# Rotary halves 32 partitions apart: swapping them with ScalarE copies out of PSUM instead of SBUF DMAs, with the products in natural token order

## Chip, cores, metric

The kernel runs as one program on the 8 cores of a Trainium2 chip; each core owns 2048 of 16384 tokens. The metric is the device time in microseconds (us) of the slowest core. Some executions fall into a slow state, in which one die runs at a visibly lower granted clock (0.81 to 0.96 instead of 0.98) and takes up to 18% longer. The engines are TensorE (PE), VectorE (DVE), ScalarE (ACT), GpSimd (POOL) and SyncE (SP, which only issues DMAs here).

## The reference, cut to what matters

```python
def apply_partial_rope(t, cos, sin):          # first 32 of 128 head dims
    half = ROT_DIM // 2                        # 16
    t1, t2, rest = t[..., :half], t[..., half:ROT_DIM], t[..., ROT_DIM:]
    return jnp.concatenate([t1 * cos - t2 * sin, t1 * sin + t2 * cos, rest], axis=-1)
...
q = apply_partial_rope(q.reshape(B, S, N_QKV_HEADS, HEAD_DIM), cos, sin)
k = apply_partial_rope(k.reshape(B, S, N_QKV_HEADS, HEAD_DIM), cos, sin)
# 3 groups of 8 heads; dilations 1, 4, 16; windows of 128 strided keys
```

The rest (norm, modulation, dilated attention, gated convolution, output projection) is untouched.

## The kernel before

A core first makes the values (called the first stage below), then projects and rotates the keys of the 2048 tokens in front of its own (the **halo stage**), then does its own heads with their attention (the **own stage**), then convolution and output. Head dims lie on partitions, tokens on the free axis. Rotation needs the two halves of 16 dims exchanged, so that both factors of a product lie on the same partitions; the kernel before exchanges them by two SBUF-to-SBUF DMAs per call:

```python
# kernel before, cut
def rope(pv, g, buf, off, T, n, tab, tc, rings, lag=2):
    R = DIL[g]                                   # 1, 4, 16
    if g == 2:
        dv = buf.all()                           # four token blocks T, one dependency
        dap = buf.ap.rearrange("p (r m) -> p r m", r=16)[:, :, 32 * T:32 * T + 32]
    ...
    S.op("act", copy(out=dap, in_=iv(pv.ap)), reads=[pv], writes=[dv])               # cast
    S.op("dve", t1 = pv[0:32] * table[0:32], reads=[pv, tv], writes=[t1])            # first product
    S.dmas("sp", [(sw[32:48], dap[16:32]), (sw[48:64], dap[0:16])], reads=[dv], writes=[sw])
    def tail():                                  # two slots later
        S.op("dve", t2 = sw[32:64] * table[32:64], ...)                              # second product
        S.op("pool", dap[0:32] = t1 + t2, reads=[t1, t2], writes=[dv])               # add
    at(clock[0] + lag, 0, tail)
```

`iv` and `fv` view tokens in residue order (all tokens with the same remainder by the dilation together), the order in which the attention wants them. Dependencies are kept per 256-byte cell of the views named in `reads` and `writes`.

The host plans the order of each engine's instructions. It simulates all engines with estimated durations (`op_cost`; for DMAs an issue time plus about 2.1 us) and emits each engine's list in the simulated order of start. Each engine then has its instructions in that order, so an estimate that is off can make it wait at one instruction while later ones are ready.

```python
if nd.nbytes:
    issue = (0.55 if e == "pool" else 0.1) * len(nd.items)   # planner: us per DMA issued
```

The softmax here doesn't subtract the row's maximum and nothing guards it: scores larger than these inputs give would overflow.

Of the kernel before, what the change touches and what calls it, by code (L numbers as in the profile page):

```python
# [6 lines left out]
F32 = mybir.dt.float32  # L7
# [272 lines left out]
def op_cost(eng, fn):  # L280
    p = Probe()
    fn(p)
    name, k = p.got
    if eng == "pe":
        n = _free(k["rhs"]) if "rhs" in k else 128
        c = max(n, 120) / 2.4e3 + 0.004
        if name == "matmul" and k["rhs"].dtype == F32:
            c *= 4
        return c
    out = k["out"]  # L290
    ins = [v for key, v in k.items() if key in ("in_", "in0", "in1") and v is not None]
    n = max(_free(a) for a in ins)
    ps = any("PS" in str(a.space) for a in ins + [out])
    ptr = any(hasattr(k.get(key), "ap") for key in ("scale", "bias", "scalar", "scalar1"))
    far = n > 64 and any(len(a.ap) > 2 and a.ap[-1][0] not in (0, 1) for a in ins + [out])
    if eng == "act":
        return (n + (190 if ps else 240)) / 1.2e3 + (0.1 if ptr else 0.0)
    if eng == "pool":
        return (2.5e-3 if far or out.shape[0] > 32 else 2.2e-3) * n + 0.1
    f = 1.0  # L300
    if name in ("tensor_copy", "tensor_scalar"):
        b2 = all(a.dtype == BF16 for a in ins + [out])
        f = 1.0 if ps else (4.0 if b2 else 2.0)
    elif name == "tensor_tensor" and not ps and all(a.dtype == BF16 for a in ins + [out]):
        f = 1.5
    elif name == "reciprocal":
        f = 0.167
    if n < 16:
        return 0.26
    return (n / f * (1.5 if far else 1.0) + 151) / 0.96e3 + (0.05 if ptr else 0.0)  # L310
# [10 lines left out]
class Sched(Emit):  # L321
# [66 lines left out]
    def _plan(self):  # L388
# [26 lines left out]
        while count < len(nodes):  # L415
            best = None
            for e in ENGS:
                o = order[e]
                h = head[e]
                while h < len(o) and done[o[h]]:  # L420
                    h += 1
                head[e] = h
                cand = None
                seen = 0
                j = h
                win = self.WIN[e]
                while j < len(o) and seen < win:
                    nd = nodes[o[j]]
                    j += 1
                    if done[nd.idx]:  # L430
                        continue
                    seen += 1
                    if nd.left:
                        continue
                    st = max(free[e], nd.ready)
                    if nd.nbytes:
                        st = max(st, dma_free - 5.0)
                    k = (st, nd.idx if e == "pe" else nd.need, nd.idx)
                    if cand is None or k < cand[0]:
                        cand = (k, nd)  # L440
                if cand is not None and (best is None or (cand[0][0], cand[1].need) < (best[0][0], best[1].need)):
                    best = cand
            (st, _, _), nd = best
            e = nd.eng
            nd.start = st
            done[nd.idx] = True
            count += 1
            if nd.nbytes:
                issue = (0.55 if e == "pool" else 0.1) * len(nd.items)
                free[e] = st + issue  # L450
                b = max(dma_free, st + issue + 1.0)
                dma_free = b + max(nd.nbytes / 340e3, 0.1)
                end = dma_free + 1.0
            else:
                end = st + nd.cost
                free[e] = end
                end += 0.15
            for j in nd.succs:
                s = nodes[j]
                s.left -= 1  # L460
                if s.ready < end:
                    s.ready = end
# [57 lines left out]
def build_program():  # L520
    nc = bass.Bass("TRN2", target_bir_lowering=False)
    xt_d = nc.dram_tensor("xt", [8, 128, 16 * 512], F32, kind="ExternalInput").ap()
    crow_d = nc.dram_tensor("crow", [128, D], F32, kind="ExternalInput").ap()
    pos_d = nc.dram_tensor("pos64", [64, HALO + TOK], I32, kind="ExternalInput").ap()
    cf_d = nc.dram_tensor("cstf", [128, NCF], F32, kind="ExternalInput").ap()
    cb_d = nc.dram_tensor("cstb", [128, NCB], F32, kind="ExternalInput").ap()
    wada_d = nc.dram_tensor("wada", [3, 16, 128, D], F32, kind="ExternalInput").ap()
# [35 lines left out]
    with ExitStack() as st:  # L563
# [39 lines left out]

        stage = [S.buf(TL + 32768 + 4096 * i, [4, 4, 128], BF16) for i in range(2)]
        stats = [S.buf(TL + 40960 + 256 * i, [8], F32) for i in range(4)]
        tkv = S.buf(TL, [TOK], F32, parts=64)
        NW = 3
        wring = [S.buf(TL + 4096 * i, [KC, 128], BF16) for i in range(NW)]
        hring = wring + [S.buf(TL + 28672 + 4096 * i, [KC, 128], BF16) for i in range(3)]
# [1 line left out]
        def wslot(j):  # L611
            return hring[j % 6] if j < 24 else wring[j % NW]

        tab_o = S.buf(TL + 12288, [TOK], F32, parts=64)
        tab_h = S.buf(TL + 20480, [HALO], F32, parts=64)
        t1s = [S.buf(TL + 20480 + 2048 * i, [512], F32, parts=32) for i in range(3)]
        t2s = [S.buf(TL + 26624, [512], F32, parts=32), S.buf(R1 + 63232, [512], F32, parts=32)]
        sws = [S.buf(TL + 28672 + 1024 * i, [512], BF16, parts=64) for i in range(3)]
        zw = S.buf(TL + 31744, [KC, 128], BF16)
        F1, F2, F3 = [S.buf(TL + 35840 + 2048 * i, [512], F32) for i in range(3)]  # L620
        kth = [S.buf(R0 + 5376 * i, [2688], BF16) for i in range(2)]
        t1h = [S.buf(R0 + 10752 + 2048 * i, [512], F32, parts=32) for i in range(4)]
        t2h = [S.buf(R0 + 18944 + 2048 * i, [512], F32, parts=32) for i in range(4)]
        swh = [S.buf(R0 + 27136 + 1024 * i, [512], BF16, parts=64) for i in range(4)]
        q2 = S.buf(R1, [TOK], BF16)
        k2 = S.buf(R1 + 4096, [TOK], BF16)
        kh2 = [S.buf(R1 + 8192 + 1024 * i, [4, 128], BF16) for i in range(2)]
# [386 lines left out]
        def table_steps(tb, p0):  # L1014
# [8 lines left out]
                         reads=[in_, cf.all()], writes=[out])  # L1023
                steps.append(f)
            steps.append(lambda: S.dma("pool", tb.ap, pos_d[:, p0:p0 + 2048], writes=[sv]))
            ts(sv, sv, cf.ap[0:64, CF_INVF:CF_INVF + 1], None, ALU.mult)
            ts(kv, sv, inv2pi, MAGIC, ALU.mult, ALU.add)
            ts(kv, kv, MAGIC, None, ALU.subtract)
            for Cc in (C1, C2):
                steps.append(lambda Cc=Cc: S.op("dve", lambda e: e.scalar_tensor_tensor(  # L1030
                    out=sv.ap, in0=kv.ap, scalar=-Cc, in1=sv.ap, op0=ALU.mult, op1=ALU.add), reads=[kv, sv], writes=[sv]))
            ts(sv, sv, PI_LO, -PI_LO, ALU.min, ALU.max)
            steps.append(lambda: S.op("act", lambda e: e.activation(out=tb.ap, in_=tb.ap, func=AF.Sin, scale=cf.ap[0:64, CF_SC:CF_SC + 1]),
                                      reads=[sv, cf.all()], writes=[sv]))
            cv = View(tb.ap[0:32, :], "sb", tb.lo, tb.hi)
            steps.append(lambda: S.op("dve", lambda e: e.tensor_tensor(out=cv.ap, in0=cv.ap, in1=cv.ap, op=ALU.mult), reads=[cv], writes=[cv]))
            ts(cv, cv, -2.0, 1.0, ALU.mult, ALU.add)
            return steps
# [53 lines left out]

        rope_n = [0]

        def rope(pv, g, buf, off, T, n, tab, tc, rings, lag=2):
            T1, T2, SW = rings
            i = rope_n[0]
            rope_n[0] += 1
            t1, t2, sw = T1[i % len(T1)].v((0, n)), T2[i % len(T2)].v((0, n)), SW[i % len(SW)].v((0, n))
            R = DIL[g]  # L1100
            if g == 2:
                dv = buf.all()
                dap = buf.ap.rearrange("p (r m) -> p r m", r=16)[:, :, 32 * T:32 * T + 32]
            else:
                dv = buf.v((off, off + n))
                dap = dv.ap.rearrange("p (r m) -> p r m", r=R)

            def iv(ap):
                return ap.rearrange("p (m r) -> p r m", r=R)

            def fv(ap):
                return ap.rearrange("p (r m) -> p r m", r=R)
            tv = tab.v((tc, tc + n))
            S.op("act", lambda e: e.copy(out=dap, in_=iv(pv.ap)), reads=[pv], writes=[dv])  # L1114
            S.op("dve", lambda e: e.tensor_tensor(out=fv(t1.ap), in0=iv(pv.ap[0:32, :]), in1=iv(tv.ap[0:32, :]), op=ALU.mult),  # L1115
                 reads=[pv, tv], writes=[t1])
            S.dmas("sp", [(fv(sw.ap[32:48, :]), dap[16:32]), (fv(sw.ap[48:64, :]), dap[0:16])], reads=[dv], writes=[sw])

            def tail():
                S.op("dve", lambda e: e.tensor_tensor(out=fv(t2.ap), in0=fv(sw.ap[32:64, :]), in1=iv(tv.ap[32:64, :]), op=ALU.mult),  # L1120
                     reads=[sw, tv], writes=[t2])
                S.op("pool", lambda e: e.tensor_tensor(out=dap[0:32], in0=fv(t1.ap), in1=fv(t2.ap), op=ALU.add),  # L1122
                     reads=[t1, t2], writes=[dv])
            at(clock[0] + lag, 0, tail)

        ringh = (t1h, t2h, swh)
        for h in range(8):
            kb = kth[h % 2]
            kb2 = S.buf(kb.lo, [HALO], BF16)
# [191 lines left out]
                at(C + 3, 4, lambda u=u: fin3(u))  # L1321

        ringo = (t1s, t2s, sws)
        assert clock[0] == 0
        for h in range(8):
            attn_head(h)
            for g, qb, kb, ko in ((2, q2, k2, 0), (0, q0, k0, 128), (1, q1, k1, 512)):
                for which, buf, off in ((0, qb, 0), (24, kb, ko)):
                    wb = w_get(("in", which + g * 8 + h))
                    for T in range(4):  # L1330
                        a, b = 512 * T, 512 * T + 512
                        pv = proj(wb, lambda kc: own(T, kc))
                        lag = 2 if clock[0] < 190 else 191 - clock[0]
                        rope(pv, g, buf, off + a, T, 512, tab_o, a, ringo, lag)
                        tick()
        assert clock[0] == 192

# [244 lines left out]
```

## Time and profile before

| | before |
|---|---|
| time, 3 runs | 3777.9 us median (3777.86 to 3786.51); a fourth, with the changed kernel's runs, 3798.72 |
| halo stage, slowest core | 211 us, PE idle 48, clock 0.90 |
| own stage, slowest core | 1025 us, PE idle 45 |

The page's summary of the engines (busy us, share of the span, instructions) and the last line, the chain of work that ended last, with each engine's share of the span:

```profile
PE 3527.4 (93%) x17640; PEld 1650.4 (44%) x17640; DVE 1509.6 (40%) x2013; ACT 817.2 (22%) x1380; POOL 714.7 (19%) x803
...
PE 74%; DMA 14%; DVE 3%; issue 3%; POOL 2%; ACT 2%; SPq 1%; DVEq 0%; POOLq 0%; ACTq 0%
```

PE carries the time, but 14% of the chain runs through DMAs. That is where to look for time that isn't arithmetic. Groups, waits and timeline of this kernel stand in the prediction.

### The profile page before, as it was taken

The numbers are of one execution on the slowest core, as the hardware profiler recorded it, in microseconds if no ns is written. First come the engines' busy times: TensorE is split into PE (matmuls) and PEld (weight loads), VectorE is DVE, ScalarE is ACT, GpSimd is POOL, SyncE is SP. The second block draws the span as 40 slices with busy tenths as digits, with TensorE's granted clock in tenths as the row PEclk, the third lists the DMA queues.
The fourth block names the chain that finished last, engine by engine and source line by source line (L and its number), as shares of the span: only waits on it lengthen the run. The fifth ranks groups of instructions, "written<-read, shape, count | busy, mean of one in ns | idle before, by whom it ended". The sixth has DMA issues, their size and how long they took to land.

```text
span 3776.1 us, 51795 instructions; the slowest of 8 cores (3749.5 to 3776.1 us)
## 1 busy us (share of the span) xinstructions
PE 3527.4 (93%) x17640; PEld 1650.4 (44%) x17640; DVE 1509.6 (40%) x2013; ACT 817.2 (22%) x1380; POOL 714.7 (19%) x803
## 2 busy tenths in 40 slices
PE   6779998779999999999999999999999999999994
PEld 2334454334544444444444444444444444444441
DVE  4868103445666656665543221111242323111113
ACT  4576311112332223222200001001210000110021
POOL 4741002333322233332000000000100000000010
PEclk9989999899999999999999999999999999999997
DMA  9996413443333333333664444444895444444478
GB/s 226 194 223 137 88 39 79 86 96 68 74 69 65 75 70 74 65 69 71 169 159 74 77 73 77 78 75 78 164 214 98 74 77 76 77 77 78 74 131 216
DMA packets 228330, 385.56 MB, mean 102 GB/s; under 512 B 107876, under 2 KB 140004, under 8 KB 221544
## 3 DMA queue, kind: packets, MB, share of 16 engines
q0 software_dynamic: 67120, 236.29, 38.0%
q1 hardware_dynamic: 160232, 143.87, 13.0%
q8 instruction: 146, 2.39, 0.3%
q10 hardware_dynamic: 720, 2.10, 0.2%
q14 instruction: 112, 0.92, 0.1%
HBM read 569.32 MB, written 40.38 MB: 161 GB/s over the span
## 4 chain that ended last, share of the span: by engine, by line
PE 74%; DMA 14%; DVE 3%; issue 3%; POOL 2%; ACT 2%; SPq 1%; DVEq 0%; POOLq 0%; ACTq 0%
PE pb L1073 62%; PE pb L990 7%; DMA arena<-arena 6%; PE pb L1158 4%; DMA arena<-xt 3%; DMA vs<-arena 2%; DMA arena<-wada 2%; POOL arena L1122 1%; SPq L208 1%; PE pb L788 1%; DMA out<-arena 1%; DVE arena L1120 1%; DMA arena<-wo 1%; ACT arena L1114 1%; DVE arena L1115 1%
## 5 line engine op out<-in xcount | busy, mean ns | idle before, releaser
L1073 PE MATMUL pb<-arena 128*128 128x512 bf16 (+1 forms) x13568 | 2879.3, 372 | 70.7 <-DVE arena L1115 55.1
L1073 PEld LDWEIGHTS pb<-arena 128*128 128x128 bf16 x13568 | 1284.8, 98 | 1592.1 <-issue 127.9
L1122 POOL TENSOR_TENSOR arena<-arena 32x512 bf16<-32x512 f32 x240 | 326.8, 1364 | 715.9 <-DMA arena<-arena 298.5
L208 POOL DMA_DIRECT2D arena<-win x280 | 150.5, 538 | 1413.0 <-PE pb L1073 1066.3
L1120 DVE TENSOR_TENSOR arena<-arena 32x512 f32<-32x512 bf16 x240 | 241.5, 1015 | 358.6 <-DMA arena<-arena 281.9
L1452 DVE TENSOR_TENSOR arena<-pb,arena 128x512 f32<-128x512 f32 x128 | 88.5, 692 | 635.4 <-ACT arena L1451 635.4
L788 PE MATMUL pb<-arena 128*128 128x512 bf16 x1024 | 248.7, 403 | 79.0 <-DMA arena<-xt 35.6
L1114 ACT CAST arena<-pb 128x512 bf16<-128x512 f32 x240 | 135.1, 575 | 697.9 <-PE pb L1073 337.3
L990 PE MATMUL pb<-arena 128*128 128x512 bf16 x1184 | 255.7, 379 | 0.0
L1115 DVE TENSOR_TENSOR arena<-pb,arena 32x512 f32<-32x512 f32 x240 | 217.7, 910 | 91.7 <-ACT arena L1114 57.1
L1451 ACT ACTIVATE arena<-pb 128x512 f32<-128x512 f32 x128 | 76.4, 597 | 681.8 <-PE pb L1073 681.7
L1158 PE MATMUL pb<-arena 128*128 128x128 bf16 (+2 forms) x1632 | 183.0, 266 | 37.3 <-DVE arena L1154 36.6
L788 PEld LDWEIGHTS pb<-arena 128*128 128x128 bf16 x1024 | 102.4, 102 | 221.0 <-issue 121.1
L990 PEld LDWEIGHTS pb<-arena 128*128 128x128 bf16 x1184 | 125.7, 106 | 129.9
L1158 PEld LDWEIGHTS pb<-arena 128*128 128x128 bf16 x1632 | 131.9, 104 | 104.4 <-issue 62.4
L1426 ACT ACTIVATE arena<-pb 128x512 f32<-128x512 f32 x64 | 38.2, 597 | 576.4 <-PE pb L1073 576.4
L721 DVE SCALAR_TENSOR_TENSOR arena<-arena 128x2048 f32<-128x2048 f32 x48 | 116.1, 2422 | 72.6 <-DMA arena<-wada 72.1
L763 POOL TENSOR_TENSOR arena<-arena 128x512 f32<-128x512 f32 (+2 forms) x88 | 133.8, 1523 | 46.7 <-DVE arena L755 23.0
L1401 DVE TENSOR_TENSOR arena<-pb,arena 128x512 f32<-128x512 f32 x64 | 44.3, 692 | 240.1 <-PE pb L1073 240.0
L1152 ACT ACTIVATE arena<-pb 128x512 bf16<-128x512 f32 x192 | 108.0, 600 | 19.2 <-PE pb L1158 17.5
L1429 DVE TENSOR_TENSOR arena<-arena 128x512 bf16<-128x512 f32 x64 | 44.2, 691 | 168.4 <-ACT arena L1426 168.4
L924 DVE SCALAR_TENSOR_TENSOR pb<-arena 128x512 f32<-128x512 bf16 x128 | 96.5, 815 | 17.5 <-ACT arena L926 16.9
(81 smaller groups left out, 1352.4 us busy)
## 6 DMA issues: line engine op xcount, KB each, us to landing
arena<-win POOLq DMA_DIRECT2D x280, 512.0 KB, 5.7
arena<-wada SPq DMA_DIRECT2D x48, 1024.0 KB, 7.6
arena<-wo POOLq DMA_DIRECT2D x64, 512.0 KB, 6.3
arena<-xt POOLq DMA_DIRECT2D x32, 512.0 KB, 9.7
arena<-xt SPq DMA_DIRECT2D x64, 256.0 KB, 6.2
arena<-wco POOLq DMA_DIRECT2D x32, 512.0 KB, 5.2
out<-arena SPq DMA_DIRECT2D x64, 256.0 KB, 6.4
arena<-wv POOLq DMA_DIRECT2D x24, 512.0 KB, 10.1
```

Of the source, the lines that this page charges most:

```text
L208: return e.dma_start(out=out, in_=in_)
L721: S.op("dve", lambda e: e.scalar_tensor_tensor(out=w.ap, in0=w.ap, scalar=1.0, in1=cr.ap, op0=ALU.mult, op1=ALU.mult, accum_out=mr), reads ...
L763: S.op("pool", lambda e, a=a, k=k, o=o: e.tensor_tensor(out=o.ap, in0=a.ap, in1=b.ap[:, k, :], op=ALU.add), reads=[a, b.v(k)], writes=[o])
L788: S.op("pe", lambda e, kc=kc, l=l: e.matmul(pv.ap, lhsT=l.ap, rhs=wb.ap[:, kc, :], start=(start and kc == k0), stop=(stop and kc == k1 - 1 ...
L990: S.op("pe", lambda e, kc=kc, l=l, pv=pv: e.matmul(pv.ap, lhsT=l.ap, rhs=wb.ap[:, kc, :], start=(kc == 0), stop=(kc == KC - 1)), reads=[l, ...
L1073: S.op("pe", lambda e, kc=kc, r=r: e.matmul(pv.ap, lhsT=wb.ap[:, kc, :], rhs=r.ap, start=(kc == 0), stop=(kc == nk - 1)), reads=[wb.v(kc), ...
L1114: S.op("act", lambda e: e.copy(out=dap, in_=iv(pv.ap)), reads=[pv], writes=[dv])
L1115: S.op("dve", lambda e: e.tensor_tensor(out=fv(t1.ap), in0=iv(pv.ap[0:32, :]), in1=iv(tv.ap[0:32, :]), op=ALU.mult), reads=[pv, tv], write ...
L1120: S.op("dve", lambda e: e.tensor_tensor(out=fv(t2.ap), in0=fv(sw.ap[32:64, :]), in1=iv(tv.ap[32:64, :]), op=ALU.mult), reads=[sw, tv], wri ...
L1122: S.op("pool", lambda e: e.tensor_tensor(out=dap[0:32], in0=fv(t1.ap), in1=fv(t2.ap), op=ALU.add), reads=[t1, t2], writes=[dv])
L1152: S.op("act", lambda e: e.activation(out=p.ap, in_=pb.ap, func=AF.Exp, scale=scale_qk), reads=[pb], writes=[p.all()])
L1158: S.op("pe", lambda e: e.matmul(out, lhsT=lhs, rhs=rhs, start=start, stop=stop, skip_group_check=True), reads=reads, writes=[bankv], signa ...
```

## The change

The host permutes the weight columns of q and k so that the halves come out of the projection on partitions 0 to 15 and 32 to 47. Then ACT exchanges them straight out of PSUM: one copy reads from partition 32 on and writes from 64 on, the other reads from 0 and writes from 96. The products read and write tokens in natural order, without strides; the add on POOL scatters its result into residue order. The planner's figure for a DMA issue on SP or ACT is corrected from 0.1 to 0.6 us.

```diff
-                issue = (0.55 if e == "pool" else 0.1) * len(nd.items)
+                issue = (0.55 if e == "pool" else 0.6) * len(nd.items)
...
-            S.op("dve", lambda e: e.tensor_tensor(out=fv(t1.ap), in0=iv(pv.ap[0:32, :]), in1=iv(tv.ap[0:32, :]), op=ALU.mult),
-            S.dmas("sp", [(fv(sw.ap[32:48, :]), dap[16:32]), (fv(sw.ap[48:64, :]), dap[0:16])], reads=[dv], writes=[sw])
-            def tail():
-                S.op("dve", lambda e: e.tensor_tensor(out=fv(t2.ap), in0=fv(sw.ap[32:64, :]), in1=iv(tv.ap[32:64, :]), op=ALU.mult),
-                S.op("pool", lambda e: e.tensor_tensor(out=dap[0:32], in0=fv(t1.ap), in1=fv(t2.ap), op=ALU.add),
-            at(clock[0] + lag, 0, tail)
+            for lo, so in ((32, 64), (0, 96)):
+                S.op("act", lambda e, lo=lo, so=so: e.copy(out=sw.ap[so:so + 16, :], in_=pv.ap[lo:lo + 16, :]), reads=[pv], writes=[sw])
+            S.op("dve", lambda e: e.tensor_tensor(out=t1.ap, in0=pv.ap[0:48, :], in1=tv.ap[0:48, :], op=ALU.mult), ...)
+            S.op("dve", lambda e: e.tensor_tensor(out=t2.ap, in0=sw.ap[64:112, :], in1=tv.ap[64:112, :], op=ALU.mult), ...)
+            S.op("pool", lambda e: e.tensor_tensor(out=dap[0:48].rearrange("p r m -> p m r"), in0=nat(t1.ap), in1=nat(t2.ap), op=ALU.add), ...)
...
+    rot = np.r_[0:16, 32:48, 16:32, 48:128]
+    win_r[:48] = win_r[:48].reshape(48, 128, KC, 128)[..., rot].reshape(48, 128, KC * 128)
```

Cut: tables and buffers on 112 or 48 partitions instead of 64 or 32, seven memsets of the swap buffers, and a planner cost for them. With `tail` the delay of two slots goes, too.

More of the change, by code (lines that the diff above doesn't have):

```diff
@@ L289, in op_cost @@
         return c
+    if name == "memset":
+        return 0.7
     out = k["out"]
@@ L523, in build_program @@
     crow_d = nc.dram_tensor("crow", [128, D], F32, kind="ExternalInput").ap()
-    pos_d = nc.dram_tensor("pos64", [64, HALO + TOK], I32, kind="ExternalInput").ap()
+    pos_d = nc.dram_tensor("pos112", [112, HALO + TOK], I32, kind="ExternalInput").ap()
     cf_d = nc.dram_tensor("cstf", [128, NCF], F32, kind="ExternalInput").ap()
@@ L605, in build_program @@
         stats = [S.buf(TL + 40960 + 256 * i, [8], F32) for i in range(4)]
-        tkv = S.buf(TL, [TOK], F32, parts=64)
+        tkv = S.buf(TL, [TOK], F32, parts=112)
         NW = 3
@@ L612, in wslot @@
             return hring[j % 6] if j < 24 else wring[j % NW]
-        tab_o = S.buf(TL + 12288, [TOK], F32, parts=64)
-        tab_h = S.buf(TL + 20480, [HALO], F32, parts=64)
-        t1s = [S.buf(TL + 20480 + 2048 * i, [512], F32, parts=32) for i in range(3)]
-        t2s = [S.buf(TL + 26624, [512], F32, parts=32), S.buf(R1 + 63232, [512], F32, parts=32)]
-        sws = [S.buf(TL + 28672 + 1024 * i, [512], BF16, parts=64) for i in range(3)]
+        tab_o = S.buf(TL + 12288, [TOK], F32, parts=112)
+        tab_h = S.buf(TL + 20480, [HALO], F32, parts=112)
+        t1s = [S.buf(TL + 20480 + 2048 * i, [512], F32, parts=48) for i in range(3)]
+        t2s = [S.buf(TL + 26624, [512], F32, parts=48), S.buf(R1 + 63232, [512], F32, parts=48)]
+        sws = [S.buf(TL + 28672 + 1024 * i, [512], BF16, parts=112) for i in range(3)]
         zw = S.buf(TL + 31744, [KC, 128], BF16)
@@ L621, in build_program @@
         kth = [S.buf(R0 + 5376 * i, [2688], BF16) for i in range(2)]
-        t1h = [S.buf(R0 + 10752 + 2048 * i, [512], F32, parts=32) for i in range(4)]
-        t2h = [S.buf(R0 + 18944 + 2048 * i, [512], F32, parts=32) for i in range(4)]
-        swh = [S.buf(R0 + 27136 + 1024 * i, [512], BF16, parts=64) for i in range(4)]
+        t1h = [S.buf(R0 + 10752 + 2048 * i, [512], F32, parts=48) for i in range(4)]
+        t2h = [S.buf(R0 + 18944 + 2048 * i, [512], F32, parts=48) for i in range(4)]
+        swh = [S.buf(R0 + 27136 + 1024 * i, [512], BF16, parts=112) for i in range(4)]
         q2 = S.buf(R1, [TOK], BF16)
@@ L1025, in table_steps @@
             steps.append(lambda: S.dma("pool", tb.ap, pos_d[:, p0:p0 + 2048], writes=[sv]))
-            ts(sv, sv, cf.ap[0:64, CF_INVF:CF_INVF + 1], None, ALU.mult)
+            ts(sv, sv, cf.ap[0:112, CF_INVF:CF_INVF + 1], None, ALU.mult)
             ts(kv, sv, inv2pi, MAGIC, ALU.mult, ALU.add)
@@ L1032, in table_steps @@
             ts(sv, sv, PI_LO, -PI_LO, ALU.min, ALU.max)
-            steps.append(lambda: S.op("act", lambda e: e.activation(out=tb.ap, in_=tb.ap, func=AF.Sin, scale=cf.ap[0:64, CF_SC:CF_SC + 1]),
+            steps.append(lambda: S.op("act", lambda e: e.activation(out=tb.ap, in_=tb.ap, func=AF.Sin, scale=cf.ap[0:112, CF_SC:CF_SC + 1]),
                                       reads=[sv, cf.all()], writes=[sv]))
-            cv = View(tb.ap[0:32, :], "sb", tb.lo, tb.hi)
+            cv = View(tb.ap[0:48, :], "sb", tb.lo, tb.hi)
             steps.append(lambda: S.op("dve", lambda e: e.tensor_tensor(out=cv.ap, in0=cv.ap, in1=cv.ap, op=ALU.mult), reads=[cv], writes=[cv]))
@@ L1093, in build_program, with rope @@
         rope_n = [0]
-        def rope(pv, g, buf, off, T, n, tab, tc, rings, lag=2):
+        def rope(pv, g, buf, off, T, n, tab, tc, rings):
             T1, T2, SW = rings
@@ L1106, in rope, with nat @@
                 dap = dv.ap.rearrange("p (r m) -> p r m", r=R)
-            def iv(ap):
-                return ap.rearrange("p (m r) -> p r m", r=R)
-            def fv(ap):
-                return ap.rearrange("p (r m) -> p r m", r=R)
+            def nat(ap):
+                return ap.rearrange("p (m r) -> p m r", r=R)
             tv = tab.v((tc, tc + n))
-            S.op("act", lambda e: e.copy(out=dap, in_=iv(pv.ap)), reads=[pv], writes=[dv])
-            S.op("dve", lambda e: e.tensor_tensor(out=fv(t1.ap), in0=iv(pv.ap[0:32, :]), in1=iv(tv.ap[0:32, :]), op=ALU.mult),
-                 reads=[pv, tv], writes=[t1])
-            S.dmas("sp", [(fv(sw.ap[32:48, :]), dap[16:32]), (fv(sw.ap[48:64, :]), dap[0:16])], reads=[dv], writes=[sw])
-            def tail():
-                S.op("dve", lambda e: e.tensor_tensor(out=fv(t2.ap), in0=fv(sw.ap[32:64, :]), in1=iv(tv.ap[32:64, :]), op=ALU.mult),
-                     reads=[sw, tv], writes=[t2])
-                S.op("pool", lambda e: e.tensor_tensor(out=dap[0:32], in0=fv(t1.ap), in1=fv(t2.ap), op=ALU.add),
-                     reads=[t1, t2], writes=[dv])
-            at(clock[0] + lag, 0, tail)
+            S.op("act", lambda e: e.copy(out=dap, in_=pv.ap.rearrange("p (m r) -> p r m", r=R)), reads=[pv], writes=[dv])
+            for lo, so in ((32, 64), (0, 96)):
+                S.op("act", lambda e, lo=lo, so=so: e.copy(out=sw.ap[so:so + 16, :], in_=pv.ap[lo:lo + 16, :]), reads=[pv], writes=[sw])
+            S.op("dve", lambda e: e.tensor_tensor(out=t1.ap, in0=pv.ap[0:48, :], in1=tv.ap[0:48, :], op=ALU.mult), reads=[pv, tv], writes=[t1])
+            S.op("dve", lambda e: e.tensor_tensor(out=t2.ap, in0=sw.ap[64:112, :], in1=tv.ap[64:112, :], op=ALU.mult), reads=[sw, tv], writes=[t2])
+            S.op("pool", lambda e: e.tensor_tensor(out=dap[0:48].rearrange("p r m -> p m r"), in0=nat(t1.ap), in1=nat(t2.ap), op=ALU.add),
+                 reads=[t1, t2], writes=[dv])
         ringh = (t1h, t2h, swh)
+        for b in swh:
+            S.op("pool", lambda e, b=b: e.memset(b.ap[64:112, :], 0.0), writes=[b.all()])
         for h in range(8):
@@ L1323, in build_program @@
         ringo = (t1s, t2s, sws)
+        for b in sws:
+            S.op("pool", lambda e, b=b: e.memset(b.ap[64:112, :], 0.0), writes=[b.all()])
         assert clock[0] == 0
@@ L1332, in build_program @@
                         pv = proj(wb, lambda kc: own(T, kc))
-                        lag = 2 if clock[0] < 190 else 191 - clock[0]
-                        rope(pv, g, buf, off + a, T, 512, tab_o, a, ringo, lag)
+                        rope(pv, g, buf, off + a, T, 512, tab_o, a, ringo)
                         tick()
@@ L1561 @@
         cstf[:, CF_CONVW:CF_CONVW + 48] = cw.T.reshape(16, 128, 3).transpose(1, 0, 2).reshape(128, 48)
-        cstf[0:64, CF_INVF] = np.tile(inv_freq, 4)
-        cstf[0:32, CF_SC] = 0.5
-        cstf[32:48, CF_SC] = -1.0
-        cstf[48:64, CF_SC] = 1.0
+        for lo, sc in ((0, 0.5), (32, 0.5), (64, -1.0), (96, 1.0)):
+            cstf[lo:lo + 16, CF_INVF] = inv_freq
+            cstf[lo:lo + 16, CF_SC] = sc
         cstf[:, CF_ONE] = 1.0
@@ L1573 @@
         in_maps.append({
-            "xt": xt, "crow": crow, "pos64": np.ascontiguousarray(np.broadcast_to(p[None, :], (64, HALO + TOK))),
+            "xt": xt, "crow": crow, "pos112": np.ascontiguousarray(np.broadcast_to(p[None, :], (112, HALO + TOK))),
             "cstf": cstf, "cstb": cstb, "wada": wada_r, "win": win_r, "wv": wv_r, "wao": wao_r, "wco": wco_r, "wo": wo_r,
```

## The prediction

> **What bounds the kernel now.** I read the page first: its engine lines, then its costliest groups. TensorE (PE) is busy 93% of 3776.1 us; VectorE (DVE) 40%, ScalarE (ACT) 22%, GpSimd (POOL) 19%. So an operation that gets cheaper on another engine is worth only the PE waiting that it ends. There are 240 rotary calls (rope), 48 on halo keys and 192 on the core's own q and k. Four groups of the page are theirs:
>
> ```profile
> L1122 POOL TENSOR_TENSOR arena<-arena 32x512 bf16<-32x512 f32 x240 | 326.8, 1364 | 715.9 <-DMA arena<-arena 298.5
> L1120 DVE TENSOR_TENSOR arena<-arena 32x512 f32<-32x512 bf16 x240 | 241.5, 1015 | 358.6 <-DMA arena<-arena 281.9
> L1114 ACT CAST arena<-pb 128x512 bf16<-128x512 f32 x240 | 135.1, 575 | 697.9 <-PE pb L1073 337.3
> L1115 DVE TENSOR_TENSOR arena<-pb,arena 32x512 f32<-32x512 f32 x240 | 217.7, 910 | 91.7 <-ACT arena L1114 57.1
> ```
>
> See the last column: the second product (L1120) and the POOL add (L1122) sat idle some 280 and 300 us until a swap DMA (arena<-arena) landed.
>
> Next I read the busy times in two stretches, cut at 805 us, where the first bias matmul (L1192) opens the core's own heads:
>
> ```profile
> 594.00:805.00 211.00, 163.18 (x758) 72.24 (x757) 91.86 (x88) 21.97 (x44) 67.36 (x64) 0.90 0.48 93
> 805.00:1830.00 1025.00, 980.33 (x5598) 496.25 (x5596) 614.22 (x798) 292.78 (x524) 308.08 (x268) 1.00 0.35 69
> ```
>
> Length, then PE, PE loads, DVE, ACT, POOL busy, granted clock, DMA share, GB/s. In the halo stage PE is idle for 48 of 211 us and its clock averages 0.90; in the own stage it is idle for 45 of 1025 us at clock 1.00. After 1830 us PE is nearly always full. The waits of the halo stage, then PE's own waits in the whole run:
>
> ```profile
> ACT arena L1114 <- DMA arena<-arena: 150.4, 16, 13.7
> POOL arena L1122 <- DMA arena<-arena: 131.4, 15, 12.0
> DVE arena L1120 <- DMA arena<-arena: 114.1, 24, 10.0
> ...
> PE pb L1073 <- DVE arena L1115: 55.1, 16, 7.3
> ```
> ```profile
> PE pb L1073 <- DVE arena L1115: 55.1, 16, 7.3
> PE pb L1158 <- DVE arena L1154: 36.6, 26, 2.6
> ```
>
> All 55.1 us of the first wait lie in the halo stage: a projection waits for a PSUM bank until the first product (L1115) has read it. Why that is late, the timeline tells:
>
> ```profile
> 720.88 0.59 ACT L1114 CAST arena<-pb 128x512 bf16<-128x512 f32 x1 [12.21 <-DMA arena<-arena]
> ...
> 721.99 0.99 DVE L1115 TENSOR_TENSOR arena<-pb,arena 32x512 f32<-32x512 f32 x1
> ...
> 723.13 13.26 PE L1073 MATMUL pb<-arena 128*128 128x512 bf16 x48 [5.51 <-DVE arena L1115]
> ```
>
> The cast waited 12.2 us for a DMA, the product followed, PE idled 5.5 us. The code says why: for group 2 the four token blocks of a head count as one buffer (dv = buf.all()), so the cast of block T+1 may not start until the swap DMA of T has read and the POOL add of T has written. The same pattern returns at 749.58 us: 28.7 us a head.
>
> The second wait is the attention's: numerators wait for the masked exponentials (L1154). One case:
>
> ```profile
> 1051.08 1.25 POOL L1122 TENSOR_TENSOR arena<-arena 32x512 bf16<-32x512 f32 x1 [5.04 <-DMA arena<-arena]
> 1052.42 1.07 ACT L1114 CAST arena<-pb 128x512 bf16<-128x512 f32 x2 [6.09 <-POOL arena L1122]
> ...
> 1053.38 1.11 ACT L1152 ACTIVATE arena<-pb 128x512 bf16<-128x512 f32 x2
> ...
> 1054.41 0.74 DVE L1154 TENSOR_TENSOR arena<-arena 128x512 bf16<-128x512 bf16 x2
> ...
> 1054.96 1.89 PE L1158 MATMUL pb<-arena 128*128 128x128 bf16 x10 [1.35 <-DVE arena L1154]
> ```
>
> The swap was late, so add, cast, exponential (behind the cast in ACT's order), mask and PE were. I went through the 26 waits of this core: in about two thirds DVE or ACT had just stood still for a swap or the add behind it; the others follow a full DVE queue.
>
> **What the Trainium skill says.** "DMA: Bandwidth & Descriptors", section Anatomy of one DMA, puts about 2.0 us of fixed cost on any transfer, most of it confirmation of the write. The trace agrees at best: the DMA list has 2.1 us median for the 464 swaps of 16 KB, but 4.4 us in the halo stage. "VectorE: DVE Perf Modes", section The TRN2 errata, gives a fp32 two-tensor product of N elements (N+151)/0.96, 691 ns at 512. The plain product L1401 agrees (692 ns); the rope's strided ones do not (1.00 to 1.06 us), its unstrided ones do (0.68). "GPSIMD Engine Reference", section Key points, says POOL shares its SBUF interfaces with DVE operations that read two SBUF inputs; 14 of the 240 L1120 took 2.1 us, seen beside POOL adds. "TensorE: Matmul & The Clock Gate", section The HAM clock gate, says that about 3.4 us of idling lowers the clock; here gaps of 5 us go with 0.83 in most 20 us slices of the halo stage.
>
> **The change part by part.**
> Removed: 480 swap DMAs, SP issues at about 0.6 us each (two took 1.24 us) and 2.1 to 4.4 us of landing out of every chain, most of the DMA packets under 512 B, and the two-slot delay before a rope's tail.
> Added: two ACT copies of 16 partitions out of PSUM per rope. By the cast's durations (585 ns at 512 columns, 285 at 128): 464 x 0.585 + 16 x 0.285 = 276 us of ACT. Over a halo head that makes ACT busy for about 9 of 18 us, over the own stage 293 + 192 x 1.17 = 518 of 1000 us. It has room. The planner orders ACT by need, so exponentials go ahead of copies; a copy already running delays one by at most 0.59 us.
> Cheaper: both products lose their strides. At 0.69 us: 232 x 0.69 + 8 x 0.3 = 162 us each against 217.7 and 241.5; say 110 us less DVE after some contention.
> Dearer: the POOL add spans 48 partitions and scatters its output. No row shows that form; my allowance is 1.4 to 1.9 us for the present 1.26.
> Small: 7 memsets, tables on 112 partitions for 64 (same columns, so about the same time), host reordering that the device doesn't see, and a planner that now reckons 0.6 us per SP issue, which can reorder DMAs anywhere.
>
> **Halo stage.** The new chain of group 2: the copies do not touch dv and can go before the cast, so from one cast to the next there are cast 0.59, first product 0.69, add 1.4, three handovers of about 0.1: 3.0 us. A 512-column projection takes 3.45 us (the chain lists it so: 16 matmuls). 3.0 < 3.45, so PE sets the pace; even an add of 1.9 us gives 3.5, and heads overlap by the two key buffers. PE's work is 40 x 3.45 + 8 x 0.9 (the 128-column projections: a burst of two wide ones and a narrow one took 7.96) = 145 us, at clock 1.00 because the gaps go. With 5 us for start and late handovers 150, against 211: **61 us less**. The weight loads: 3 a head at 5.7 us to landing, prefetched up to six deep; the DMA engines, 48% busy over 28 us a head, would be about 65% busy over 18 without the swaps.
>
> **Own stage.** Of 36.6 us of mask waits I take two thirds as ended, 24; the other idling stays. About **25 us less**. The rest: 0, plus or minus 6 for the planner's reordering.
>
> Sum: 3777.9 - 61 - 25 = **3692 us**, 2.3% less.
>
> **Rivals.**
> (1) ACT takes the DMA's place: three PSUM reads in a row, and the first product waits for the cast in ACT's queue. For it: attention has exponentials, casts and logs on one in-order engine, and mask waits could stay at 37 us. Against: 52% load, and each copy is short. Then own gains 0 to 5 us: about 3712.
> (2) POOL becomes the chain: scattered writes at 48 partitions at 2.5 us or more make 4.1 us from cast to cast, over PE's 3.45, and hold the two t2 buffers. For it: adds have taken up to 2.1 us beside DVE. Against: inputs become contiguous. Halo would stay near 165 us, the total near 3715.
> (3) The halo stage meets its weights: 3 loads in 18 us for 28 before, on chips where all eight cores load at once. For it: landing is 6.2 us there already. Against: the prefetch depth. It would return 10 us: 3702.
> (4) Everything hidden anyway. Against it stand 55 us of PE waits with their DMA cause in the timeline.
>
> **Range and chances.** If all idling of both stages went, 61 + 5 + 45 would be saved: 3667, the floor. Rivals 1 and 2 together give about 3735, unlikely. Eight in ten: 3672 to 3718. 2% faster means under about 3703; the centre is 11 us below it, my spread some 18 us, so 0.73 for faster, 0.26 for the same, 0.01 for slower.
>
> **What would show it.** Halo stage right: 150 us from first key projection to first bias matmul, granted clock near 1.00, hardly any PE wait on the first product. Own stage: mask waits near 12 us, DVE near 510 us, ACT near 520. Products at 0.69 us, new copies near 0.58, add 1.4 to 1.9. The prediction is wrong if the ACT copies or the add turn up as what PE's waits end on, if weight loads (arena<-win) end PE's waits in the halo stage, or if the stages before 594 or after 1830 us move by more than 6 us.

## The result

The first four timed runs of the changed kernel gave 4303.27, 3982.25, 3683.85 and 3683.48 us; the first two are slow-state runs (clock 0.82 and 0.90 on one die). Two more fast runs gave 3686.32 and 3683.71. Fast against fast the ratio is **0.9733** (95% interval 0.9702 to 0.9765): 2.7% faster. A repeat on another chip gave 0.9723, with fast runs of 3680.92 to 3690.11 us. A ratio is the mean of one kernel's fast runs over the mean of the other's fast runs of the same rounds, so it is not quite the ratio of the medians that are quoted.

The page of the changed kernel: the engines, the chain, then the rope's groups.

```profile
PE 3511.2 (95%) x17640; PEld 1647.8 (45%) x17640; DVE 1453.5 (39%) x2013; ACT 1092.4 (30%) x1860; POOL 870.6 (24%) x810
...
PE 80%; DMA 10%; POOL 3%; DVE 3%; ACT 2%; issue 2%; SPq 0%; ACTq 0%; DVEq 0%; POOLq 0%
...
L1118 POOL TENSOR_TENSOR arena<-arena 48x512 bf16<-48x512 f32 x240 | 501.1, 2094 | 436.2 <-DVE arena L1117 310.0
...
L1115 ACT CAST arena<-pb 16x512 bf16<-16x512 f32 x480 | 270.5, 563 | 222.3 <-PE pb L1075 205.4
...
L1116 DVE TENSOR_TENSOR arena<-pb,arena 48x512 f32<-48x512 f32 x240 | 160.4, 668 | 218.8 <-ACT arena L1115 144.8
L1117 DVE TENSOR_TENSOR arena<-arena 48x512 f32<-48x512 bf16 x240 | 218.9, 915 | 39.7 <-ACT arena L1115 33.5
...
L1113 ACT CAST arena<-pb 128x512 bf16<-128x512 f32 x240 | 138.3, 576 | 169.8 <-POOL arena L1118 166.7
```

No DMA ends an idle time of these groups any more; DMA fell from 14% to 10% of the chain. ACT gained 275 us, as reckoned: the 16-partition copies took 574 ns at 512 columns, which agrees with the estimate of 570 ns by "VectorE: DVE Perf Modes", section The TRN2 errata, whose table has 172 + 512 cycles at 1.2 GHz for a ScalarE operation from PSUM. But the add grew from 1364 to 2094 ns on the mean, and the casts still wait 167 us for it. The first product got cheaper (910 to 668 ns), the second hardly (1015 to 915).

Halo and own stage of the slowest core (length, then PE, PE loads, DVE, ACT, POOL busy, granted clock, DMA share, GB/s):

```profile
599.00:751.00 152.00, 146.34 (x761) 68.91 (x760) 93.68 (x90) 70.92 (x135) 103.48 (x70) 1.00 0.55 113
751.00:1733.00 982.00, 976.16 (x5598) 495.60 (x5596) 556.60 (x797) 516.86 (x914) 434.59 (x269) 1.00 0.33 67
```

The halo stage took 152 us instead of 211, the own stage 982 instead of 1025. Of the 59 us of the halo stage, 42 are idle time of PE (48 to 6). The other 17 are PE's busy time (163 to 146 us), at a granted clock of 1.00 instead of 0.90. PE's own waits on the first product and on the masks:

```profile
PE pb L1075 <- DVE arena L1116: 5.9, 10, 1.0
...
PE pb L1155 <- DVE arena L1151: 4.6, 9, 1.2
```

They were 55.1 and 36.6 us. What is left of the halo chain shows in the timeline of the changed kernel (start, duration, instruction, idle before it):

```profile
649.56 2.47 POOL L1118 TENSOR_TENSOR arena<-arena 48x512 bf16<-48x512 f32 x1 [1.73 <-DVE arena L1116]
650.00 2.06 DVE L1117 TENSOR_TENSOR arena<-arena 48x512 f32<-48x512 bf16 x1 [0.65 <-ACT arena L1115]
652.12 0.59 ACT L1113 CAST arena<-pb 128x512 bf16<-128x512 f32 x1 [2.36 <-POOL arena L1118]
...
652.81 0.68 DVE L1116 TENSOR_TENSOR arena<-pb,arena 48x512 f32<-48x512 f32 x1 [0.74 <-ACT arena L1113]
...
653.70 2.47 POOL L1118 TENSOR_TENSOR arena<-arena 48x512 bf16<-48x512 f32 x1 [1.66 <-DVE arena L1116]
...
656.25 0.59 ACT L1113 CAST arena<-pb 128x512 bf16<-128x512 f32 x1 [2.29 <-POOL arena L1118]
```

Cast, product, add, next cast: 656.25 - 652.12 = 4.13 us per block, over the 3.45 us of a projection. And the second product at 650.00 us lasts 2.06 instead of 0.69 us, ending together with the POOL add that runs beside it.

### The profile page after: what moved, and what is told of

It reads as the page before. It is cut to its first block, busy times and chain, and to the rows that moved or that the text cites. A ratio compares the mean times of both kernels' runs of the same rounds, so it can differ in the third digit from the quotient of the medians.

```text
span 3682.3 us, 50338 instructions; the slowest of 8 cores (3652.2 to 3682.3 us)
## 1 busy us (share of the span) xinstructions
PE 3511.2 (95%) x17640; PEld 1647.8 (45%) x17640; DVE 1453.5 (39%) x2013; ACT 1092.4 (30%) x1860; POOL 870.6 (24%) x810
## 4 chain that ended last, share of the span: by engine, by line
PE 80%; DMA 10%; POOL 3%; DVE 3%; ACT 2%; issue 2%; SPq 0%; ACTq 0%; DVEq 0%; POOLq 0%
PE pb L1075 68%; PE pb L992 7%; PE pb L1155 4%; DMA arena<-xt 3%; DMA vs<-arena 2%; DMA arena<-wada 2%; POOL arena L1118 2%; DMA out<-arena 1%; PE pb L790 1%; DVE arena L1116 1%; DMA arena<-wo 1%; POOL arena L765 1%; DVE arena L1117 1%; ACT arena L1113 0%; DVE arena L1151 0%
## 5 line engine op out<-in xcount | busy, mean ns | idle before, releaser
L1118 POOL TENSOR_TENSOR arena<-arena 48x512 bf16<-48x512 f32 x240 | 501.1, 2094 | 436.2 <-DVE arena L1117 310.0
L1115 ACT CAST arena<-pb 16x512 bf16<-16x512 f32 x480 | 270.5, 563 | 222.3 <-PE pb L1075 205.4
L1116 DVE TENSOR_TENSOR arena<-pb,arena 48x512 f32<-48x512 f32 x240 | 160.4, 668 | 218.8 <-ACT arena L1115 144.8
L1117 DVE TENSOR_TENSOR arena<-arena 48x512 f32<-48x512 bf16 x240 | 218.9, 915 | 39.7 <-ACT arena L1115 33.5
L1151 DVE TENSOR_TENSOR arena<-arena 128x512 bf16<-128x512 bf16 x192 | 121.1, 649 | 50.9 <-ACT arena L1149 50.3
```

What stands on the lines that cost most here:

```text
L1115: S.op("act", lambda e, lo=lo, so=so: e.copy(out=sw.ap[so:so + 16, :], in_=pv.ap[lo:lo + 16, :]), reads=[pv], writes=[sw])
L1116: S.op("dve", lambda e: e.tensor_tensor(out=t1.ap, in0=pv.ap[0:48, :], in1=tv.ap[0:48, :], op=ALU.mult), reads=[pv, tv], writes=[t1])
L1117: S.op("dve", lambda e: e.tensor_tensor(out=t2.ap, in0=sw.ap[64:112, :], in1=tv.ap[64:112, :], op=ALU.mult), reads=[sw, tv], writes=[t2])
L1118: S.op("pool", lambda e: e.tensor_tensor(out=dap[0:48].rearrange("p r m -> p m r"), in0=nat(t1.ap), in1=nat(t2.ap), op=ALU.add), reads=[t1 ...
L1151: S.op("dve", lambda e: e.tensor_tensor(out=pap, in0=pap, in1=mask_ap, op=ALU.mult), reads=[p.all(), cb.all()], writes=[p.all()])
```

## The experiments

All kernels gave correct results. Stage lengths are means over the eight cores of the profiled run, cut at the last value matmul, the first bias matmul and the last attention matmul. "Mask waits" is PE's waiting (pieces over 0.15 us) ahead of attention matmuls, mean of the cores. Ratio: to the kernel before of the same rounds, whose fast runs had medians of 3782 to 3788 us there and not 3777.9; so compare ratios, not times of different rows.

| kernel | swap | planner SP | T blocks of group 2 | halo | own | mask waits | fast runs, median us | ratio [95%] |
|---|---|---|---|---|---|---|---|---|
| before | DMA | 0.1 | one buffer | 211 | 1026 | 36 | 3777.9 | 1 |
| planner only | DMA | 0.6 | one buffer | 179 | 1001 | 8 | 3730.4 | 0.984 [0.981, 0.987] |
| regions only | DMA | 0.1 | four regions | 147 | 1018 | 31 | 3708.2 | 0.981 [0.978, 0.983] |
| regions + planner | DMA | 0.6 | four regions | 145 | 977 | 4 | 3670.6 | 0.970 [0.968, 0.973] |
| changed | ACT, natural | 0.6 | one buffer | 152 | 981 | 5 | 3684.3 | 0.972 [0.969, 0.975] |
| changed, planner back | ACT, natural | 0.1 | one buffer | 153 | 981 | 5 | 3679.8 | 0.972 [0.969, 0.974] |
| changed, POOL cost right | ACT, natural | 0.6 | one buffer | 150 | 972 | 1 | 3671.3 | 0.970 [0.962, 0.978] |
| changed, regions | ACT, natural | 0.6 | four regions | 145 | 971 | 1 | 3670.6 | 0.970 [0.967, 0.973] |
| residue order | ACT, residue | 0.6 | one buffer | 145 | 971 | 1 | 3665.6 | 0.967 [0.964, 0.970] |
| residue order, regions | ACT, residue | 0.6 | four regions | 145 | 971 | 1 | 3665.5 | 0.969 [0.964, 0.974] |
| changed, copies twice | ACT x2, natural | 0.6 | one buffer | 160 | 999 | 19 | 3709.1 | 0.980 [0.974, 0.985] |

(For "changed, regions" the profile fell in a slow state; its stages are those of the four cores of the undisturbed die. It and "POOL cost right" have two fast runs each. The intervals of "planner only", "regions only" and "copies twice" exclude 1, but none of the three is shown to gain 2%: the record's verdicts are same, unclear, unclear.)

**The theories.** Mine, from the prediction: the swap DMAs were the cost, through the chain of group 2 and through late exponentials, so taking them away is the gain. Rivals: the planner's number, changed on the side, did it; the cheaper DVE products did it; or the one-buffer dependency was the cost and the DMA harmless.

### The changed kernel again

> The changed kernel again, as the yardstick of the runs beside it. Expected as on record: fast runs near 3684 us, stages (means over the cores) of about 596 us before the halo keys, 152 halo, 981 own heads, 1941 after.

Measured: ratio 0.9723; stages 592, 152, 981, 1941 us. As expected.

### Planner's number alone on the kernel before

```diff
-                issue = (0.55 if e == "pool" else 0.1) * len(nd.items)
+                issue = (0.55 if e == "pool" else 0.6) * len(nd.items)
```

> The kernel before with one number changed: the host planner reckons 0.6 us instead of 0.1 us per DMA issued on SP or ACT. Theory P (the planner's number reorders the instructions of the first stage, and this is why that stage grew from 585 to 596 us in the changed kernel): first stage near 595 us, and with the other stages as before (211, 1026, 1939) a total near 3788 us. Rival C (the 11 us are chance, or come from elsewhere in the change): first stage 585 plus or minus 4, total within 4 us of the kernel before. Side question: if a better plan of the swap DMAs were worth much of the gain, the halo and own stages would shrink by 10 us or more here; I expect less than 10.

Measured: ratio 0.984, 1.6% faster without touching the rope. I had expected under 10 us from the two stages and got 58 (1237.6 against 1179.5, before rounding). Its stages, in the same columns as above:

```profile
594.00:773.00 179.00, 145.75 (x713) 66.15 (x712) 85.56 (x82) 21.87 (x43) 63.50 (x60) 0.93 0.54 98
773.00:1774.00 1001.00, 982.62 (x5635) 501.19 (x5634) 632.56 (x804) 294.03 (x525) 315.67 (x272) 1.00 0.37 73
```

The DMAs themselves did not get quicker (median landing in the own stage 2.3 us, 2.0 before), but PE's mask waits fell from 36 to 8 us. The likely reason, not shown, is that with about the right issue time the lists place the work that waits for a swap so that less stands behind it. So on the kernel before, over half of the gain was to be had by one number of the host's model. The first stage, which the runs also were to settle, came to 592 us.

### Planner's number put back in the changed kernel

```diff
-                issue = (0.55 if e == "pool" else 0.6) * len(nd.items)
+                issue = (0.55 if e == "pool" else 0.1) * len(nd.items)
```

> The changed kernel with the planner's number put back to 0.1 us. Theory P: first stage back near 585 us, halo 152 and own 981 unchanged, total near 3673 us, some 0.3% under the changed kernel. Rival C: first stage stays near 596 us and the total within 4 us of the changed kernel.

Measured: 3679.8 us; in the mean 3 us or 0.09% under the repeat of the changed kernel in the same rounds; stages 595, 153, 981. Theory P fell. Where no swap DMA is left, the planner's figure for SP is worth nothing. The two runs together show that its gain does not add to that of the copies.

### The kernel before, profiled once more

> The kernel before once more, for a second profile of its first stage. Theory C (the first stage varies from run to run): its mean over the cores lies near 592 us, as in every later run, not at the 584.6 us of the first profile. Theory D (something in the change lengthens it): near 585 us again. Halo 211 and own 1026 as before.

Measured: first stage 591 us (582 to 596 by core), halo 213, own 1025. Theory C holds: across all profiles, in both orders of the planner, the first stage lay between 585 and 601 us. The 11 us that it was longer in the changed kernel (585 to 596) lie within what varies from run to run; nothing shows them to be part of the change.

### ScalarE copies kept, residue order restored

The edit, abridged:

```diff
-  S.op("act", copy(out=sw[so:so+16], in_=pv[lo:lo+16]))
-  S.op("dve", t1 = pv[0:48] * tv[0:48])                       # natural order
-  S.op("dve", t2 = sw[64:112] * tv[64:112])
-  S.op("pool", dap[0:48].rearrange("p r m -> p m r") = nat(t1) + nat(t2))
+  S.op("act", copy(out=fv(sw[so:so+16]), in_=iv(pv[lo:lo+16])))
+  S.op("dve", fv(t1) = iv(pv[0:48]) * iv(tv[0:48]))           # residue order
+  S.op("dve", fv(t2) = fv(sw[64:112]) * iv(tv[64:112]))
+  S.op("pool", dap[0:48] = fv(t1) + fv(t2))
```

> The changed kernel with the ScalarE copies kept but the products and the add in residue order, as before: both VectorE products strided (about 1.0 us for groups 1 and 2), the GpSimd add contiguous (about 1.3 us at 48 partitions instead of 2.5). Theory S (the swap DMAs out of the chain are the gain; the order of the products gives nothing to PE): halo 150 us or less since the chain from cast to cast falls from 4.1 to 3.2 us, own 981 to 986, total 3678 to 3688. Rival N (the cheaper VectorE products emptied the queue in front of the masks): mask waits return to 12 us or more and the own stage to 995 us or more, total 3698 or more.

Measured: 3665.6 us, with "residue order, regions" the fastest; in the same rounds its mean is 3666.0 us against 3684.9 for the changed one, 0.5% less. Its groups on the page:

```profile
L1121 POOL TENSOR_TENSOR arena<-arena 48x512 bf16<-48x512 f32 x240 | 296.6, 1237 | 517.6 <-DVE arena L1120 364.9
...
L1119 DVE TENSOR_TENSOR arena<-pb,arena 48x512 f32<-48x512 f32 x240 | 218.3, 912 | 129.6 <-ACT arena L1118 116.8
...
L1120 DVE TENSOR_TENSOR arena<-arena 48x512 f32<-48x512 bf16 x240 | 240.9, 1006 | 48.0 <-ACT arena L1118 42.1
```

The add costs 1237 ns on 48 partitions: the partitions cost nothing, the scatter doubled it. DVE is as slow as before the change, yet PE is idle for 0.2 us of the halo stage and 2.7 of the own stage. Theory S holds, and beyond what I expected of it (971 instead of 981 to 986): the natural order does not bring the gain, it takes away some 17 us (7 in the halo stage, 10 in the own stage), as long as the dependency and the planner's cost of the add stay as they are.

### The kernel before with four regions

The blocks T of a group 2 head interleave in memory in pieces of 64 bytes. The edit, abridged, names each block's own cells. It also keeps all other dependencies per 64 bytes instead of 256, which no run separates:

```diff
-CELL = 256
+CELL = 64
...
-                dv = buf.all()
+                dv = Part(buf.ap, "sb", buf.lo, buf.hi)
+                dv.cells = [(buf.lo + 256 * r + 64 * T) // CELL for r in range(16)]
```

> The kernel before, swap DMAs and planner number untouched, but the four token blocks of a group 2 head tracked as four regions instead of one buffer, so that the cast of a block no longer waits for the swap and the add of the block before. Theory W (this chain bounds the halo stage): halo 165 us or less against 211, own 1010 or less against 1026, total 3725 or less. Rival Q (the SP queue takes the swaps in a badly planned order, and the chain is secondary): halo 190 or more, total 3755 or more.

Measured: halo 147 us, own 1018, ratio 0.981; halo as theory W expects, and the total below its bound, own not (1018 against 1010). PE's waits on the masks and on the first product, slowest core:

```profile
PE pb L1165 <- DVE arena L1161: 40.0, 23, 4.5
...
PE pb L1078 <- DVE arena L1122: 5.6, 6, 3.1
```

The wait that cost the halo stage its time is gone with the swap DMAs still there. The mask waits are not (31 us in the mean of the cores); the planner's number alone had ended most of them.

### Four regions and planner's number, swap DMAs kept

> The same with the planner's 0.6 us per SP issue as well: the swap DMAs stay, but neither chained nor misplanned. If the swap DMAs were a cost only through these two, halo is 155 us or less, own 990 or less and the total 3700 or less, near the changed kernel. If their landing time itself holds the rings of three and two scratch buffers, halo stays at 165 or more or own at 1000 or more.

Measured: 3670.6 us, ratio 0.970. The kernel before, with all 480 swap DMAs, strided products and the two-slot delay, is as fast as the changed one or a little faster. Its stages, and its swaps in the list of DMA issues (count, KB each, us to landing):

```profile
603.00:748.00 145.00, 145.00 (x760) 69.26 (x759) 85.75 (x91) 24.69 (x46) 63.10 (x66) 1.00 0.69 130
748.00:1725.00 977.00, 971.47 (x5587) 495.80 (x5585) 634.14 (x795) 292.23 (x522) 293.25 (x266) 1.00 0.37 73
```
```profile
arena<-arena SPq DMA_DIRECT2D x464, 16.0 KB, 2.5
```

The second product still sat idle for 181 us until swaps landed, but PE no longer did. So the DMAs' own latency was not the cost, except for at most 6 us of the own stage (977 against 971 of the residue-order kernel); a chain that did not exist in the data, and a plan that reckoned wrongly, were. My theory of the swap DMAs as the cost falls in that form.

### Changed kernel with four regions

The same edit on the changed kernel.

> The changed kernel with the four token blocks tracked as four regions. Theory K (the scattered add of 2.5 us makes the cast to cast chain 4.1 us, longer than a projection's 3.45): without the chain halo falls from 152 to 146 or 147 with PE idle under 1 us; own gains 3 us or less, because there VectorE operations held beside GpSimd adds remain. Rival V (VectorE held beside GpSimd costs PE its time in the halo stage too): halo stays at 150 or more.

Measured: halo 145, own 971 on the undisturbed die; fast runs 3668.5 and 3672.7 us. Stages of one of its cores:

```profile
603.00:748.00 145.00, 145.00 (x768) 69.61 (x767) 69.87 (x93) 73.61 (x139) 105.59 (x74) 1.00 0.62 129
748.00:1719.00 971.00, 970.46 (x5588) 497.43 (x5586) 505.63 (x793) 513.27 (x910) 430.59 (x266) 1.00 0.33 66
```

Theory K holds for the halo stage. For the own stage I was wrong: I had expected 3 us or less and got 10. The scattered add costs as much POOL time as in the changed kernel (431 us against 435), but once no cast waits for it, it costs PE nothing.

### Planner told the real cost of the add

```diff
-        return (2.5e-3 if far or out.shape[0] > 32 else 2.2e-3) * n + 0.1
+        return (4.65e-3 if far else 2.5e-3 if out.shape[0] > 64 else 2.25e-3) * n + 0.1
```

> The changed kernel with the planner told the measured times of the GpSimd add (2.5 us scattered, 1.26 us contiguous) in place of 1.38 us. If the 7 us of the halo stage and the 10 us of the own stage that the scattered add costs come from a plan that counts on a faster add, own falls to 975 or less. If they come from the chain of adds through one buffer, halo stays at 152 and own at 979 or more.

Measured: own 972 us, halo 150. In the own stage 9 of the 10 us came from a plan that counted on an add of 1.38 us; in the halo stage a right plan returns 3 of the 7 us, and the chain keeps the rest. The pattern of the kernel before repeats on a smaller scale: a chain, and a plan that does not know its length.

### Copies twice

```diff
-            for lo, so in ((32, 64), (0, 96)):
+            for lo, so in ((32, 64), (0, 96), (32, 64), (0, 96)):
```

> The changed kernel with each of the two ScalarE swap copies done twice into the same place: some 270 us more ScalarE work, nothing else. Theory R (ScalarE has room in both stages): halo 152 to 155, own 981 to 990, total within 12 us of the changed kernel. Rival 1 of the prediction (exponentials queue behind copies and PE waits for the masks): mask waits of 20 us or more, own 1000 or more.

Measured: ratio 0.980; halo 160, own 999, mask waits 19. Neither theory's numbers hold: 25 us in the medians instead of 12 or less, but short of rival 1's bounds of 20 and 1000. ACT's load in the slowest core:

```profile
609.00:768.00 159.00, 146.51 (x755) 68.13 (x754) 74.61 (x89) 116.36 (x224) 100.73 (x70) 1.00 0.56 115
768.00:1768.00 1000.00, 978.63 (x5602) 496.40 (x5601) 561.36 (x798) 747.16 (x1305) 448.11 (x270) 1.00 0.32 65
```

At 53% of the own stage (517 of 982 us, changed kernel) ACT's copies cost nothing that the residue-order kernel would show; at 75% (747 of 1000) they cost 18 us. The room is real for one pair of copies; where between the two it ends was not measured. Nor was it separated how much of the 18 us is ACT's load and how much the longer wait of each rope's products for its copies.

### Residue order and four regions

> Copies kept, residue order, and the four regions: all three remedies together. If halo 145 and own 971 are PE's own work, as three other kernels suggest by landing there, nothing is left to gain: the stages stay at 145 and 971, total within 6 us of the residue-order kernel.

Measured: 145 and 971 us, fast runs 3663.8 to 3669.8. Nothing left to gain: these two stages are at PE's own work.

## Why the prediction was right or wrong

- **Total and halo stage: right.** 3692 us was forecast, 3684 measured; 150 forecast for the halo stage, 152 measured, at clock 1.00 as said. The chain through the one buffer was rightly named as what bounded it: removing that dependency alone took the stage to 147 us. That the total came so close is in part luck. On the slowest cores the own stage gave 18.5 us more than forecast and the halo stage 2 less, and the first and last stages came out 5 and 4 us longer. In the mean of the cores the first stage moved by 11 us, which the prediction had named as a sign of being wrong; the kernel before moved by 7 between its two profiles.
- **The add: mis-sized.** "My allowance is 1.4 to 1.9 us": it took 2.48 for the strided groups and 1.26 for group 0. The chain was therefore 4.1 us, as in rival 2, and not 3.0. Rival 2's size was off too: it said 165 us, the stage took 152. I had said that heads overlap by the two key buffers and then did not use it there: the first cast of the next head does not wait for the last add of this one. The chain is 0.7 us too long per block, and the 7 us that the stage lies over its 145 are 0.9 us per head.
- **Own stage: mis-sized.** 25 us were forecast, 45 came. The step that failed: "two thirds" of the mask waits ended and the others, which "follow a full DVE queue", stay. In the changed kernel the mask waits fell by 30.5 us (36 to 5), PE's other idling, which was to stay, by 8, and its busy time by 6. With four regions and the right number in the planner, DVE does the same strided products (634 us busy) and the mask waits are 4 us. So DVE's load was not what filled the queues; the chain and the plan were.
- **DVE near 510 us: wrong** (557). With four regions it was 506. Of the 51 us between, the second products make 20 (786 ns in the mean against 688) and the mask products 29 (649 against 499); both read two SBUF inputs, and all 39 mask products that took over 0.5 us ended within 0.3 us of the end of a POOL add beside them. It did not matter for PE in the forecast's sum; the products' lower cost was worth nothing to PE.
- **The planner, "0, plus or minus 6": right for the changed kernel** (putting it back moved 3 us), but I took it for a detail. On the kernel before it is worth 58 us of the two stages.
- **The cause, as far as it was put on the DMAs: half right.** They stood in the chain that the timeline showed. But taking them out is only one of two ways to break it; keeping them and removing the false dependency and the wrong figure gives 3671 us.
- **Rivals.** 1 (ACT) did not happen with one pair of copies, and a cost appears with two. 3 (weights) did not: PE's waits for weight loads from the input projection came to under 2 us on the slowest core of the changed kernel.

Open: PE's busy time in the own stage is some 5 us lower in the best kernels than in the changed one (971 against 976) although they run the same matmuls; the ends of matmuls are modelled, and I did not find out what part of a wait is counted as busy. Also open is which instructions the planner's lists exchange; only the waits show its effect.

## What to carry to other kernels

When an engine waits for a transfer, ask first whether the data require the wait: a dependency kept per buffer where the pieces are disjoint, together with a static order planned on a wrong latency, can look just like a slow DMA. Repair the dependency and the model before rebuilding the data path, and test each alone; two remedies for the same wait do not add up. When an order of data is changed to unburden one engine, look at which engine pays for the rearrangement: here idle DVE time was bought with a doubled POOL add on the chain.

## What the Trainium skill lacked or had wrong

- "GPSIMD Engine Reference", section Performance pitfalls for Q7 kernels, has a figure for reads with a step over 8 bytes, but none for writes; elsewhere the skill names a penalty for accesses that step from line to line of SBUF, without its size. Here an add with contiguous reads took 2.48 us at 512 columns when it scattered its bf16 output in steps of 256 bytes, and 1.26 when it wrote contiguously. 48 partitions cost the same as 32 (1.26 us). Its section Key points names the contention with DVE; that one of the two is blocked for a whole instruction stands elsewhere in the skill, but no page has a figure for a product beside a POOL add. Here a DVE product with two SBUF inputs lasted to the end of the POOL add beside it, 2.06 us instead of 0.69; one of 128 columns took 2.45 us instead of 0.3 and ended 0.35 us before the add.
- "VectorE: DVE Perf Modes", section The TRN2 errata: its formula, stated for the fp32 add of two tensors, gives 691 ns at 512 elements and has no term for strides. The rope's products keep to it when unstrided (0.68 us); strided ones took 1.00 to 1.06 us in the kernel before.
- No page that I read says what a wrong latency in a host-planned static order costs: here 58 us of 1237 in two stages, with the DMAs themselves unchanged.
